# Operand loads, splits and tile rings in the down products of an encoder layer

## The chip, the cores and the metric

The kernel runs on one core of a Trainium2 chip. The metric is the device time of one execution in microseconds; the time before is the median of three runs. Beside the runs one execution is profiled, and every trace row in this document comes from such an execution. Engines are named as in the rows: PE is TensorE's matmul and PEld its weight load, DVE is Vector, ACT is ScalarE, POOL is GpSimd, SP is the queue from which most loads are issued.

## What is computed

One step of a hybrid encoder layer, in float32, on 1024 prompt tokens and 32 sample tokens with D = 1024. The part that the change touches is the last one, the MLP:

```
h = rms_norm(x, g_mix);  z = h @ w_in          # q, k, v, conv, gates
x = x + (sigmoid(ga) * (attn @ w_attn_out) + sigmoid(gb) * (conv @ w_conv_out)) @ w_mix_out
x = x + cross_attention(rms_norm(x, g_cross), 256 memory tokens) @ w_co
x = x + square(relu(rms_norm(x, g_mlp) @ w_up)) @ w_down      # w_up 1024 x 4096, w_down 4096 x 1024
y = rms_norm(x, g_final)
```

## The kernel before, in words

**Three matmuls for one.** Float32 accuracy is reached by parts: every operand x is split into hi, a rounded copy made by ScalarE, and lo = x − hi, made by Vector; each product is then wh·hi + wh·lo + wl·hi, three matmuls of 128 x 128 weights by 264 columns. A weight block of 128 x 1024 is loaded on the SP queue, copied by ScalarE (L131) and subtracted by Vector (L132); this happens two blocks ahead of the step that uses it (`LOOK = 2`, L125), with three buffers.

**The order of the work.** The kernel lists its work as items (`item`, L120), and a planner puts the instructions of each engine in an order, by where they stand in the list and by its own estimate of when their inputs are ready. An instruction wrapped in `pin` (L99) is kept behind the instruction of its engine that was listed just before it. Operand splits are pinned; the splits of weights and the additions of results are not.

**The down product.** It is made of Strassen-like products with seven operands, in this order: b11, t2, b21, n3, n4, n1, b22. Five of them are *half products* (`stage`): eight steps, each one column block j of the result and one half t of the 16 operand blocks; a step has 48 matmuls. The order of the steps is `steps` (j outer, t inner) or `paired` (two j for one t, then the same two for the other t). With t = 1 a result is complete and is added to the sums of x by `to_x1` (Vector, L1908, or GpSimd, L1906). The other two, b21 and n4, are *quarter products* (`stage2`): each is split once more into seven products P1, P6, P2, P7, P5, P4, P3, in this order, with two steps of 24 matmuls each, 14 steps (L2101 to L2103). The first results are kept by a copy (L2052), later ones are added (L2054, L2059).

**What a quarter product needs.** For each of eight pairs k of operand blocks, while the half product ahead of it runs (t2 for b21, n3 for n4):

- `fetch_two`: two loads of 264 KB on GpSimd's own DMA queue (L1692, L1695);
- `first_sums`: three sums on GpSimd (L1701, L1702, L1703);
- `first_split`: the operands of P1 and P7, two ScalarE copies (L1708), two Vector subtractions (L1709);
- `extra_split`: the operands of P6 and P4, one copy (L1712) and one subtraction (L1713) of full width, 128 x 528.

`prepare` lays these over the eight steps of that half product: loads of two pairs at each of the steps 0 to 3, sums one step later, first splits two steps later, extra splits at steps 5 to 7. In the quarter product itself `beside(n)` adds, to step n: the last sums on GpSimd (L1722, for P5), the splits of the second operands for P2 and P3 (`second_split2`, on Vector, L1356, or by `far_split` on GpSimd, L1676), the splits for P5 (`last_split`), and from step 5 on the loads and splits for the next half product (`pump2`, L1678; splits L1355 and L1356). In the other half products `pump2` is called at each step.

**Tiles.** 64 homes of 128 x 528 hold the operands. `free` is a queue of homes: `take_slot` takes the first, `drop` gives one back at the end. In the kernel before every home is a buffer of its own, named by its place (`Z.3`, `H.7`).

Of the kernel before, what the change touches and what calls it, by code (L numbers as in the profile page):

```python
# [40 lines left out]
def hybrid_step(ctx: ExitStack, tc: tile.TileContext, io):  # L41
# [1227 lines left out]
    def open_first():  # L1269

        closed(m_cm)
        S["l"] = ctx.enter_context(tc.tile_pool(name="first", bufs=1, reuse_waits="tile"))
        S["z"] = ctx.enter_context(tc.tile_pool(name="second", bufs=1, reuse_waits="tile"))
        for f in range(NF):
            z = zslot()
            xa[1][f] = (quarter(z, 0), quarter(z, 1))
            pool_e.dma_start(xa[1][f][1].bitcast(F32)[:, : CH[0][1] - QT], xn_d[:, f, QT : CH[0][1]])
        for name in ("w_cq", "w_co"):
            del kept[name, 1]

    def open_sums():
        closed(cr_cm)
        closed(Y["cm", 1])
        S["s"] = ctx.enter_context(tc.tile_pool(name="sums", bufs=1, reuse_waits="tile"))
        for kind in ("t2", "n1", "n3", "n4"):
            for k in range(4):
                comb[kind, k] = tuple(at_slot(f"{kind}.{2 * k + i}") for i in range(2))
# [11 lines left out]
    def open_second():  # L1299
# [3 lines left out]
        S["b"] = ctx.enter_context(tc.tile_pool(name="b22", bufs=1, reuse_waits="tile", side="right"))  # L1303
# [3 lines left out]
    def at_slot(place, dt=F32R):  # L1307
        tag, i = place.split(".")
        pool = S[{"b22": "b", "Z": "z", "lt": "l", "H": "h"}.get(tag, "s")]
        return pool.tile([P, HT], dt, tag=tag + i, bufs=1, name=nm(tag))  # L1310

    turns = {"Z": 0, "lt": 0}

    def next_slot(tag, n, dt):
        turns[tag] += 1
        return at_slot(f"{tag}.{(turns[tag] - 1) % n}", dt)

    def zslot(dt=F32R):
        return next_slot("Z", 8, dt)

    def lslot(dt=F32):
        return next_slot("lt", 4, dt)
# [102 lines left out]
    def second_b22():  # L1425
        for k in range(4):
            comb["b22", k] = tuple(at_slot(f"b22.{2 * k + i}") for i in range(2))
# [218 lines left out]
    places = lambda text: [f"{tag}.{i}" for tag, n in (x.split("*") for x in text.split()) for i in range(int(n))]  # L1646
# [68 lines left out]
    def extra_split(kind, k):  # L1715
        cut(*take_pair(kind, ("e", k)), two["r", k])

    def last_sums(kind, m):
        two["f", m] = f = take_slot((kind, "rf", m), F32)
        for q in range(2):  # L1720
            k = 2 * m + q
            pool_e.tensor_tensor(quarter(f, q), quarter(two["x", k].bitcast(F32), 1), quarter(two["r", k], 0), op=ALU.subtract)  # L1722
            drop((kind, "r", k))
# [16 lines left out]
    def open_down():  # L1740
# [4 lines left out]
        S["h"] = ctx.enter_context(tc.tile_pool(name="hpool", bufs=1, reuse_waits="tile"))  # L1745
# [243 lines left out]
    def prepare(kind):  # L1989

        at = {n: [] for n in range(8)}
        for n in range(4):
            for k in (2 * n, 2 * n + 1):
                at[n].append(lambda k=k: fetch_two(kind, k))
                at[n + 1].append(lambda k=k: first_sums(kind, k))
                at[n + 2].append(lambda k=k: first_split(kind, k))
        for k in range(8):
            at[5 + (k + 1) // 3].append(lambda k=k: extra_split(kind, k))
        return at

    def stage(kind, w, then, q=None, each=None, more=None):
        nxt = KINDS.index(kind) + 1
        at = prepare(KINDS[nxt]) if nxt < len(KINDS) and KINDS[nxt] in RAW2 else None
        order = paired if at or kind in after2 else steps
        if nxt < len(KINDS) and not at:
            item(lambda: wanted2.extend((KINDS[nxt], k) for k in range(16)))
        for n, (j, t) in enumerate(order):

            def fn(ws, n=n, j=j, t=t):
                prod(kind, j, t, then, q)(ws)  # L2010
                if nxt < len(KINDS) and all(x[1] != t for x in order[n + 1 :]):
                    drop_pairs(kind, range(8 * t, 8 * t + 8))
                pump2(4 if n == 0 and kind in after2 else 0 if at else 3)
                for x in at[n] if at else ():
                    x()
# [8 lines left out]
        if nxt < len(KINDS):  # L2024
            item(lambda: pump2(0))

    def stage2(kind, h, f0, last):
# [46 lines left out]
        def beside(n):  # L2074
            if n < 2:
                last_sums(kind, 2 * n)
                last_sums(kind, 2 * n + 1)
            if n < 4:
                second_split2(kind, 2 * n, False)
                second_split2(kind, 2 * n + 1, n > 0)  # L2080
            elif n < 6:
                last_split(kind, 2 * n - 8)
                last_split(kind, 2 * n - 7)
            if n == 5:
                wanted2.extend((nxt, k) for k in range(16))
            if n >= 5:
                pump2({5: 2, 7: 2, 9: 2, 11: 2, 13: 4}.get(n, 0))
# [154 lines left out]
```

## Time and profile before

| what | value |
|---|---|
| runs | 1770.3, 1775.59, 1780.19 us; median 1775.59 |
| the profiled execution, its own time | 1777.22 us |
| its span in the trace | 1775.4 us |
| granted TensorE clock, mean | 0.991 |
| PE busy | 1733.3 us, 98% of the span, 12166 matmuls |
| DVE busy | 1256.8 us, 71% |
| ACT busy | 882.4 us, 50% |
| POOL busy | 773.2 us, 44% |
| the down products | 1408.5 to 1765 us |

The profiled execution's own time is 1.8 us more than its span. A row of a trace gives an instruction's start, its length, the engine, the line of the kernel, the operation, the output and inputs by their names in the program, their shapes and how many it stands for; in brackets is how long the engine stood idle just before and what it waited for. Rows that begin with an engine and end with three numbers are waits by line: total us, times, longest us. In rows with a stretch of time (A:B) come the busy time of each engine, with the number of its instructions, and the clock that TensorE was granted (1.00 is full speed).

### The profile page before, as it was taken

The page shows a single profiled execution, that of the slowest core. Times are in us where ns is not written, and L with a number is a line of the kernel's source. Part 1 is how long each engine was busy: PE and PEld are TensorE (multiplying, and loading weights), DVE is VectorE, ACT ScalarE, POOL GpSimd, SP SyncE. Part 2 cuts the span into 40 slices and gives each one's busy share as a digit, 9 for nine tenths or more (in the row PEclk, how much of TensorE's full clock was granted, in tenths as well). Part 3 has the DMA queues.
Part 4 walks back from the last instruction along what each step waited for, and adds up shares of the span by engine and source line. Part 5 has one row for each costly group of instructions (what it writes and reads, how often), then busy time and mean ns, then how long its engine had stood idle before and what let it go on. Part 6 is the DMA issues. An engine that isn't in the chain of part 4 may idle for free. (4 is left out here: it accounts for less than half of the span.)

```text
span 1775.4 us, 32859 instructions
## 1 busy us (share of the span) xinstructions
PE 1733.3 (98%) x12166; PEld 1708.7 (96%) x12166; DVE 1256.8 (71%) x2322; ACT 882.4 (50%) x1716; POOL 773.2 (44%) x901
## 2 busy tenths in 40 slices
PE   9999999999999999999999999999999999998998
PEld 8999999999999999999999999999999999897998
DVE  7776877868777546656776878686666675866785
ACT  8643534435335324434565666764444543444553
POOL 0026577664673555652324150015555315466221
PEclk9999999999999999999999999999999999998999
DMA  5334445455456888877865667756666775564944
GB/s 185 109 103 140 159 152 189 162 181 173 172 187 238 273 306 286 286 242 263 274 212 196 205 220 240 250 194 219 221 222 218 259 262 174 177 222 136 329 147 146
DMA packets 189009, 369.70 MB, mean 208 GB/s; under 512 B 19617, under 2 KB 108353, under 8 KB 188721
## 3 DMA queue, kind: packets, MB, share of 16 engines
q1 hardware_dynamic: 165232, 287.71, 48.9%
q0 software_dynamic: 22992, 79.12, 13.3%
q8 instruction: 96, 1.57, 0.4%
q10 hardware_dynamic: 624, 0.77, 0.1%
q14 instruction: 65, 0.52, 0.1%
HBM read 265.41 MB, written 101.53 MB: 207 GB/s over the span
## 5 line engine op out<-in xcount | busy, mean ns | idle before, releaser
L131 ACT CAST wh<-wr 128x1024 fp32r<-128x1024 f32 (+1 forms) x226 | 236.2, 1046 | 320.8 <-PE acc L206 82.4
L132 DVE TENSOR_TENSOR wl<-wr,wh 128x1024 fp32r<-128x1024 f32 (+1 forms) x226 | 296.3, 1312 | 99.7 <-ACT wh L131 98.7
L205 PE MATMUL acc<-X,wh 128*128 128x384 f32 (+1 forms) x864 | 281.4, 326 | 0.0
L206 PE MATMUL acc<-X,wh 128*128 128x384 f32 (+1 forms) x864 | 278.7, 323 | 0.0
L207 PE MATMUL acc<-X,wl 128*128 128x384 f32 (+1 forms) x864 | 277.8, 322 | 0.0
L206 PEld LDWEIGHTS acc<-X,wh 128*128 128x128 f32 x864 | 162.7, 188 | 1.3 <-DVE X L285 0.3
L205 PEld LDWEIGHTS acc<-X,wh 128*128 128x128 f32 x864 | 162.4, 188 | 0.8
L207 PEld LDWEIGHTS acc<-X,wl 128*128 128x128 f32 x864 | 162.4, 188 | 0.1
L205 PE MATMUL acc<-Y,wh 128*128 128x384 f32 (+1 forms) x432 | 140.6, 326 | 5.0 <-DVE ct L1093 3.5
L281 POOL TENSOR_TENSOR xacc<-xacc,ct 128x384 f32<-128x384 f32 (+1 forms) x56 | 72.8, 1303 | 160.2 <-ACT ct L279 158.5
L206 PE MATMUL acc<-Y,wh 128*128 128x384 f32 (+1 forms) x432 | 140.0, 324 | 0.2 <-DVE Y L816 0.2
L207 PE MATMUL acc<-Y,wl 128*128 128x384 f32 (+1 forms) x432 | 139.9, 324 | 0.1
L762 POOL TENSOR_TENSOR xacc<-xacc 128x256 f32<-128x256 f32 x132 | 113.6, 860 | 30.1 <-DMA xacc<-in_w_down 22.8
L762 POOL TENSOR_TENSOR ws<-ws 128x256 f32<-128x256 f32 x132 | 112.2, 850 | 29.6 <-DMA ws<-in_w_down 17.4
L131 ACT CAST PTh<-pt 128x512 fp32r<-128x512 f32 (+3 forms) x94 | 46.0, 517 | 101.8 <-PE pt L603 100.3
L205 PEld LDWEIGHTS acc<-Y,wh 128*128 128x128 f32 x432 | 81.7, 189 | 6.5 <-DVE ct L1093 4.3
L206 PEld LDWEIGHTS acc<-Y,wh 128*128 128x128 f32 x432 | 81.7, 189 | 0.9 <-DVE Y L816 0.9
L207 PEld LDWEIGHTS acc<-Y,wl 128*128 128x128 f32 x432 | 81.8, 189 | 0.4 <-DMA wl<-wl_d 0.4
L589 ACT ACTIVATE S<-S,nmx 128x257 f32<-128x257 f32 (+1 forms) x132 | 64.2, 488 | 27.6 <-DVE nmx L584 26.5
L1925 PE MATMUL acc<-n,wh 128*128 128x264 f32 x256 | 73.2, 286 | 2.5 <-DVE n L1356 2.5
L905 PE MATMUL acc<-n,wh 128*128 128x264 f32 x256 | 72.8, 284 | 1.0 <-DVE Z L1572 1.0
L907 PE MATMUL acc<-n,wl 128*128 128x264 f32 x256 | 73.0, 285 | 0.0
(628 smaller groups left out, 5833.4 us busy)
## 6 DMA issues: line engine op xcount, KB each, us to landing
wr<-in_w_up SPq DMA_DIRECT2D x53, 512.0 KB, 4.8
wr<-in_w_in SPq DMA_DIRECT2D x52, 512.0 KB, 4.2
wr<-wsum_d SPq DMA_DIRECT2D x40, 512.0 KB, 4.4
wr<-in_w_conv_out SPq DMA_DIRECT2D x24, 512.0 KB, 4.1
wr<-in_w_mix SPq DMA_DIRECT2D x24, 512.0 KB, 4.8
wr<-in_w_down SPq DMA_DIRECT2D x20, 512.0 KB, 4.6
n_d<-Z SPq DMA_DIRECT2D x32, 264.0 KB, 4.1
xacc<-in_w_down POOLq DMA_DIRECT2D x16, 512.0 KB, 3.8
```

Source lines behind the costliest of these rows:

```text
L131: act.copy(hi, src)
L132: dve.tensor_sub(lo, src, hi.bitcast(F32))
L205: pe.matmul(out, wh[:, a], hi, start=(k == 0), stop=False)
L206: pe.matmul(out, wh[:, a], lo, start=False, stop=False)
L207: pe.matmul(out, wl[:, a], hi, start=False, stop=(k == len(acts) - 1))
L281: pool_e.tensor_tensor(acc, acc, sq, op=ALU.add)
L589: act.activation(stl[:, h, : nk + 1], stl[:, h, : nk + 1], AF.Exp, scale=-1.0, bias=nmx[:, h : h + 1], accum_out=den[:, h : h + 1],)
L762: pin(pool_e.tensor_tensor(t[:, to], t[:, x], t[:, y], op=op))
L905: pe.matmul(acc, wh[:, a], hi, start=(start and k == 0), stop=False, skip_group_check=True)
L907: pe.matmul(acc, wl[:, a], hi, start=False, stop=(k == 3), skip_group_check=True)
L1925: pe.matmul(a, wh[:, s], lo, start=False, stop=False, skip_group_check=True)
```

## The change

- **Rings.** The pools `first`, `second`, `sums`, `b22` and `hpool` become rings of 4, 8, 8, 8 and 12 tiles under one tag each; a home names its ring, not its place in it, and the names of the places and their turns go away. The bytes are the same.
- **b11 in pairs.** The first half product takes the order `paired`.
- **Loads.** `prepare` issues the loads of four pairs at step 0, of two at step 1 and of two at step 2. The sums and first splits keep their steps. An extra split is done by quarters: the first quarter (128 x 264) at steps 6 and 7 of the half product, four pairs in each; the second quarter at steps 4 and 5 of the quarter product.
- **Splits ahead of results.** In t2 and n3, and in n4's and b21's successors n1 and n3, `aside`, which holds `pump2` and the work of `prepare`, is listed ahead of `prod`, and so ahead of the addition of a step's results. In the quarter products `beside(n)` is listed ahead of the next weight's split and of the results of the step.
- **In the quarter product.** The last sums are pinned; every second split of odd k goes to GpSimd (four in place of three); the splits for P5 move from steps 4 and 5 to 6 and 7; `pump2` takes its loads two by two at steps 5 and 8 to 12, none at 6, 7 and 13.

```diff
-        S["l"] = ctx.enter_context(tc.tile_pool(name="first", bufs=1, reuse_waits="tile"))
-        S["z"] = ctx.enter_context(tc.tile_pool(name="second", bufs=1, reuse_waits="tile"))
+        S["l"] = ctx.enter_context(tc.tile_pool(name="first", bufs=4, reuse_waits="tile"))
+        S["z"] = ctx.enter_context(tc.tile_pool(name="second", bufs=8, reuse_waits="tile"))
...
-        S["s"] = ctx.enter_context(tc.tile_pool(name="sums", bufs=1, reuse_waits="tile"))
+        S["s"] = ctx.enter_context(tc.tile_pool(name="sums", bufs=8, reuse_waits="tile"))
...
-                comb[kind, k] = tuple(at_slot(f"{kind}.{2 * k + i}") for i in range(2))
+                comb[kind, k] = tuple(at_slot(kind) for _ in range(2))
...
-    def at_slot(place, dt=F32R):
-        tag, i = place.split(".")
+    def at_slot(tag, dt=F32R):
         pool = S[{"b22": "b", "Z": "z", "lt": "l", "H": "h"}.get(tag, "s")]
-        return pool.tile([P, HT], dt, tag=tag + i, bufs=1, name=nm(tag))
-
-    turns = {"Z": 0, "lt": 0}
-
-    def next_slot(tag, n, dt):
-        turns[tag] += 1
-        return at_slot(f"{tag}.{(turns[tag] - 1) % n}", dt)
+        return pool.tile([P, HT], dt, tag=tag, name=nm(tag))
...
-    places = lambda text: [f"{tag}.{i}" for tag, n in (x.split("*") for x in text.split()) for i in range(int(n))]
+    places = lambda text: [tag for tag, n in (x.split("*") for x in text.split()) for _ in range(int(n))]
...
-    def extra_split(kind, k):
-        cut(*take_pair(kind, ("e", k)), two["r", k])
+    def extra_split(kind, k, q):
+        hi, lo = take_pair(kind, ("e", k)) if q == 0 else dn[kind, ("e", k)]
+        cut(quarter(hi, q), quarter(lo, q), quarter(two["r", k], q))
+        if q:
+            drop((kind, "r", k))
 
     def last_sums(kind, m):
         two["f", m] = f = take_slot((kind, "rf", m), F32)
         for q in range(2):
             k = 2 * m + q
-            pool_e.tensor_tensor(quarter(f, q), quarter(two["x", k].bitcast(F32), 1), quarter(two["r", k], 0), op=ALU.subtract)
-            drop((kind, "r", k))
+            pin(pool_e.tensor_tensor(quarter(f, q), quarter(two["x", k].bitcast(F32), 1), quarter(two["r", k], 0), op=ALU.subtract))
 
     def last_split(kind, m):
         cut(*take_pair(kind, ("f", m)), two["f", m])
...
         closed(L["cm"])
         closed(L["cm2"])
         third.update(n=0, pool=W["pool"])
-        S["h"] = ctx.enter_context(tc.tile_pool(name="hpool", bufs=1, reuse_waits="tile"))
+        S["h"] = ctx.enter_context(tc.tile_pool(name="hpool", bufs=12, reuse_waits="tile"))
 
 
     def cross_units(c):
...
     def prepare(kind):
 
         at = {n: [] for n in range(8)}
-        for n in range(4):
-            for k in (2 * n, 2 * n + 1):
-                at[n].append(lambda k=k: fetch_two(kind, k))
-                at[n + 1].append(lambda k=k: first_sums(kind, k))
-                at[n + 2].append(lambda k=k: first_split(kind, k))
-        for k in range(8):
-            at[5 + (k + 1) // 3].append(lambda k=k: extra_split(kind, k))
+
+        def do(n, fn, ks, *args):
+            at[n] += [lambda k=k: fn(kind, k, *args) for k in ks]
+
+        pairs = [range(2 * i, 2 * i + 2) for i in range(4)]
+        do(0, fetch_two, range(4))
+        do(1, fetch_two, pairs[2])
+        do(2, fetch_two, pairs[3])
+        for i in range(4):
+            do(1 + i, first_sums, pairs[i])
+            do(2 + i, first_split, pairs[i])
+        for i in range(4):
+            do(6 + i // 2, extra_split, pairs[i], 0)
         return at
 
     def stage(kind, w, then, q=None, each=None, more=None):
         nxt = KINDS.index(kind) + 1
         at = prepare(KINDS[nxt]) if nxt < len(KINDS) and KINDS[nxt] in RAW2 else None
-        order = paired if at or kind in after2 else steps
+        order = paired if at or kind in ("b11", *after2) else steps
         if nxt < len(KINDS) and not at:
             item(lambda: wanted2.extend((KINDS[nxt], k) for k in range(16)))
         for n, (j, t) in enumerate(order):
 
             def fn(ws, n=n, j=j, t=t):
+                def aside():
+                    pump2(4 if n == 0 and kind in after2 else 0 if at else 3)
+                    for x in at[n] if at else ():
+                        x()
+
+                early = at or kind in after2
+                if early:
+                    aside()
                 prod(kind, j, t, then, q)(ws)
                 if nxt < len(KINDS) and all(x[1] != t for x in order[n + 1 :]):
                     drop_pairs(kind, range(8 * t, 8 * t + 8))
-                pump2(4 if n == 0 and kind in after2 else 0 if at else 3)
-                for x in at[n] if at else ():
-                    x()
+                if not early:
+                    aside()
                 if behind and (j, t) == (1, 0):
                     behind.pop()()
 
...
                 item(lambda j=j: each(j))
             if more and (j, t) == (1, 0):
                 item(more)
-        if nxt < len(KINDS):
+        if nxt < len(KINDS) and not at:
             item(lambda: pump2(0))
 
     def stage2(kind, h, f0, last):
...
                 drop_pairs(kind, range(8, 16))
 
         def beside(n):
+            two_ks = lambda i: (2 * i, 2 * i + 1)
             if n < 2:
-                last_sums(kind, 2 * n)
-                last_sums(kind, 2 * n + 1)
+                for m in two_ks(n):
+                    last_sums(kind, m)
             if n < 4:
-                second_split2(kind, 2 * n, False)
-                second_split2(kind, 2 * n + 1, n > 0)
+                for k in two_ks(n):
+                    second_split2(kind, k, k % 2)
             elif n < 6:
-                last_split(kind, 2 * n - 8)
-                last_split(kind, 2 * n - 7)
+                for i in two_ks(n - 4):
+                    for k in two_ks(i):
+                        extra_split(kind, k, 1)
+            elif n < 8:
+                for m in two_ks(n - 6):
+                    last_split(kind, m)
             if n == 5:
                 wanted2.extend((nxt, k) for k in range(16))
             if n >= 5:
-                pump2({5: 2, 7: 2, 9: 2, 11: 2, 13: 4}.get(n, 0))
+                pump2({6: 0, 7: 0, 13: 0}.get(n, 2))
 
         n = 0
         for p in order:
...
                         pe.matmul(a, wh[:, s], hi, start=(p in start and k == 0), stop=False, skip_group_check=True)
                         pe.matmul(a, wh[:, s], lo, start=False, stop=False, skip_group_check=True)
                         pe.matmul(a, wl[:, s], hi, start=False, stop=(k == 7), skip_group_check=True)
+                    beside(n)
                     issue_w()
                     if i:
                         ended_with(p)
                     after(p, i)
-                    beside(n)
 
                 item(fn, weights[p](i))
                 n += 1
```

More of the change, by code (lines that the diff above doesn't have):

```diff
@@ L1302, in open_second @@
         closed(ps_cm)
-        S["b"] = ctx.enter_context(tc.tile_pool(name="b22", bufs=1, reuse_waits="tile", side="right"))
+        S["b"] = ctx.enter_context(tc.tile_pool(name="b22", bufs=8, reuse_waits="tile", side="right"))
         L["cm2"], L["pool2"] = opened("late2", bufs=1, reuse_waits="tile", side="right")
         ps = ctx.enter_context(tc.tile_pool(name="ps2", bufs=1, space=PSUM, reuse_waits="tile"))
-    def at_slot(place, dt=F32R):
-        tag, i = place.split(".")
+    def at_slot(tag, dt=F32R):
         pool = S[{"b22": "b", "Z": "z", "lt": "l", "H": "h"}.get(tag, "s")]
-        return pool.tile([P, HT], dt, tag=tag + i, bufs=1, name=nm(tag))
-    turns = {"Z": 0, "lt": 0}
-    def next_slot(tag, n, dt):
-        turns[tag] += 1
-        return at_slot(f"{tag}.{(turns[tag] - 1) % n}", dt)
+        return pool.tile([P, HT], dt, tag=tag, name=nm(tag))
     def zslot(dt=F32R):
-        return next_slot("Z", 8, dt)
+        return at_slot("Z", dt)
     def lslot(dt=F32):
-        return next_slot("lt", 4, dt)
+        return at_slot("lt", dt)
     def lt():
@@ L1426, in second_b22 @@
         for k in range(4):
-            comb["b22", k] = tuple(at_slot(f"b22.{2 * k + i}") for i in range(2))
+            comb["b22", k] = tuple(at_slot("b22") for _ in range(2))
             sp.dma_start(raw("b22", k), xn_d[:, k + 4, HT:])
```

## The prediction

> **What bounds the kernel now.** I read the shares of the engines first, then the busy time by stretches of the down products, then what TensorE waited for there.
>
> ```profile
> PE 1733.3 (98%) x12166; PEld 1708.7 (96%) x12166; DVE 1256.8 (71%) x2322; ACT 882.4 (50%) x1716; POOL 773.2 (44%) x901
> ```
>
> TensorE is the bound, and the change takes no matmul away: it can only win back TensorE's stalls. The stretches, in order: the start of b11, the rest of b11 with t2, the quarter product b21, n3, the quarter product n4. Behind each length stand busy time and instructions of TensorE, its weight loads, Vector, ScalarE and GpSimd, then the granted clock, the DMA engines' share and GB/s.
>
> ```profile
> 1415.70:1430.00 14.30, 11.37 (x77) 10.74 (x76) 11.87 (x14) 8.79 (x14) 3.58 (x2) 0.88 1.05 370
> 1430.00:1513.20 83.20, 83.20 (x684) 83.20 (x683) 57.68 (x127) 33.69 (x55) 30.25 (x43) 1.00 0.58 190
> 1513.20:1565.60 52.40, 46.48 (x356) 43.74 (x355) 38.19 (x54) 27.27 (x39) 19.94 (x19) 1.00 0.69 224
> 1565.60:1610.20 44.60, 44.60 (x368) 44.60 (x368) 27.68 (x42) 18.82 (x33) 31.23 (x40) 1.00 0.59 189
> 1610.20:1670.30 60.10, 49.25 (x356) 46.55 (x355) 46.18 (x66) 31.63 (x48) 29.34 (x27) 0.91 0.63 209
> ```
>
> An unbroken stretch gives the pace: 44.60 / 368 = 0.1212 us per matmul. Three stretches are longer than their matmuls: A, the start of b11, by 14.30 − 77 × 0.1212 = 5.0 us; B, b21, by 52.40 − 356 × 0.1212 = 9.25; C, n4, by 60.10 − 43.15 = 16.95. The sum, 31.2 us, is the ceiling of what this change can win; the two other stretches have no loss. What ended TensorE's waits from 1409 to 1765 us (total, times, longest):
>
> ```profile
> PE acc L2102 <- DVE lt L1709: 6.1, 1, 6.1
> PE acc L2103 <- DVE wl L132: 2.5, 7, 0.6
> PE acc L1925 <- DVE n L1356: 2.5, 2, 1.4
> PE acc L1926 <- DVE wl L132: 2.0, 3, 0.8
> PE acc L1924 <- ACT wh L131: 1.1, 1, 1.1
> PE acc L2101 <- ACT n L2052: 1.0, 1, 1.0
> PE acc L2102 <- DVE b L1713: 1.0, 1, 1.0
> PE acc L2102 <- DVE n L1356: 0.9, 1, 0.9
> ```
>
> One wait is a third of C: in the first step of n4, TensorE stood until a split of an operand of the first quarter product (L1709) was done. The second half of the loss is the clock that it left behind.
>
> ```profile
> 1425.00:1429.00 4.00, 3.53 (x17) 3.32 (x17) 3.11 (x5) 1.72 (x3) 0.00 (x0) 0.57 1.07 354
> 1621.00:1627.00 6.00, 5.80 (x26) 5.72 (x27) 6.00 (x13) 1.27 (x4) 2.63 (x3) 0.51 0.04 11
> ```
>
> ```profile
> 1619.14 0.59 PE L2102 MATMUL acc<-lt,wh 128*128 128x264 f32 x1 [6.08 <-DVE lt L1709]
> ```
>
> After 6.08 us of standing still, 26 matmuls took 6.00 us at a granted clock of 0.51 where the pace gives 3.15: 2.85 us more. In A 17 took 4.00 where 2.06 is the pace: 1.94 more, after gaps of some 1 us each.
>
> **The change, part by part.**
>
> *Operands of a quarter product fetched earlier (GpSimd).* The split that came late stands behind GpSimd's chain of n3: four issues of loads, a landing, six sums, four times over.
>
> ```profile
> 1569.23 0.57 POOL L1692 DMA_DIRECT2D H<-n_d  x1
> ...
> 1575.53 1.28 POOL L1701 TENSOR_TENSOR ct<-H,H 128x264 f32<-128x264 f32 x1 [2.89 <-DMA H<-n_d]
> ...
> 1613.60 1.18 POOL L1703 TENSOR_TENSOR Z<-b,Z 128x264 f32<-128x264 f32 x1
> ```
>
> ```profile
> POOL ct L1701 <- DMA n<-n_d: 6.2, 3, 3.6
> ```
>
> ```profile
> L1277 POOL DMA_DIRECT2D Z<-xn_d x8: 542/542/600, 1057.0 to 1060.7; - x8
> ...
> DMA to landing us min/median/max: 2.3/3.3/4.6
> ```
>
> It runs from 1569.2 to 1614.8, 45.6 us for four rounds, and in them GpSimd stands for landings, 2.89 us and 6.2 in three more: 9.1 us that it could have spent on other sums. The change issues eight loads in step 0, four in step 1, four in step 2: the same 16 issues of 0.57 us and 24 sums, but every landing after the first is now covered by a round of sums (six by 0.9 to 1.3, 5.4 to 7.8 us), and the first in part by the four issues behind it. Eight loads in a row are no risk: another line of this kernel issues eight, and the last row above has them landing in 4.6 us at most. So the chain takes 45.6 − 9.1 = 36.5 us and ends near 1605.7; the splits behind it (L1709, 0.97 us each, below) end near 1608, 2 us before n4's first matmul at 1610.2. Then the 6.1 us, the 2.85 of half clock and the wait for an L1713 split (1.0) go: **C −10**. If L2103's small waits, which stand in the half clock's stretch too, fall with it, one more; if the chain gains only half of its 9.1, it ends at 1610.2, the splits by 1613, and half of the stall is left: bounds −5 and −11. In b21 nothing is won by it: the list has no second L1709 wait.
>
> *Extra splits by quarters, and splits ahead of the results.* Vector was doing these beside the first step of n4:
>
> ```profile
> 1610.73 0.43 DVE L1709 TENSOR_TENSOR Z<-Z,n 128x264 fp32r<-128x264 f32 x1 [5.93 <-POOL lt L1702]
> ...
> 1613.49 0.69 DVE L1713 TENSOR_TENSOR t<-n,Z 128x528 fp32r<-128x528 f32 x1
> 1614.11 1.24 DVE L1713 TENSOR_TENSOR t<-n,t 128x528 fp32r<-128x528 f32 x1
> ...
> 1616.44 1.75 DVE L132 TENSOR_TENSOR wl<-wr,wh 128x1024 fp32r<-128x1024 f32 x1
> 1618.12 0.97 DVE L1709 TENSOR_TENSOR lt<-lt,b 128x264 fp32r<-128x264 f32 x1
> ```
>
> The eight extra splits (L1713) are halved in the half product (first quarter only) and the other halves move to steps 4 and 5 of the quarter product, six steps ahead of P4 which reads them; eight instructions more on ScalarE and on Vector (0.43 to 0.97 us each, as L1709 of that size), which Vector hides: it was busy 38.19 of 52.40 us in B. Each split now stands one step (24 × 0.1212 = 2.9 us) earlier, ahead of the results. The results come later by at most the splits of one step, two to four of 0.4 to 1.2 us; TensorE's wait at L2101 for one (L2052) is 1.0 us. In B this takes the waits for L1356 (0.9), the 1.0 of L2052 in part, and half of L2103's 2.5: **B −2.5**, bounds 0 and −5.
>
> *More on GpSimd in the quarter products.* Four far splits instead of three, and the eight last sums pinned to steps 0 and 1 ahead of them.
>
> ```profile
> L1676 POOL TENSOR_TENSOR n<-n,Z x2: 1861/2092/2322, 1523.2 to 1528.0; 128x528 fp32r<-128x528 f32 x2
> ...
> L1676 POOL TENSOR_TENSOR n<-n,t x1: 2692/2692/2692, 1629.4 to 1629.4; 128x528 fp32r<-128x528 f32 x1
> ```
>
> ```profile
> 1510.81 2.17 POOL L1722 TENSOR_TENSOR n<-t,t 128x264 f32<-128x264 f32 x2 [15.32 <-PE acc L1925]
> ```
>
> Two sums take 2.17 us, eight 8.7; four far splits 4 × 1.9 to 2.7 = 7.4 to 10.8: the chain is 16 to 19.5 us, and P2 wants the last of them in its first step, 4 steps and 21/24 behind the start: 14.3 us. The sums began 2.4 us ahead of the quarter product (1510.81 against 1513.2), so the last far split ends 13.6 to 17.1 us in: a new wait of 0 to 2.8 us. I take 1 in each: **+2** (0 to +5).
>
> A rule speaks against this part. L1713 of one size took 0.69 us and then 1.24, and L132 1.75 where another took 1.21 (the middle row of the next fence), while GpSimd summed. The Trainium skill, "SBUF — State Buffer", section "Who interferes with whom", has Vector and GpSimd share a port pair by an exclusive lock, so that a Vector operation with two SBUF inputs is held until GpSimd's is done. The trace shows the slowing, 1.8 times, but not a full hold of 1 to 2.7 us. By the rule each of the two more far splits would cost Vector its own length, some 2 us, and the sum would be −11; by the rows it is half of that, which the +2 has room for, and the sum goes by them.
>
> *b11 in pairs.* Its operands of half t=1 (L1355, L1356) are first read in step 2, not step 1, one step (48 × 0.1212 = 5.8 us) later. The stretch's last splits are these:
>
> ```profile
> 1421.45 3.05 DVE L1356 TENSOR_TENSOR n<-n,n 128x528 fp32r<-128x528 f32 x3
> 1424.42 1.21 DVE L132 TENSOR_TENSOR wl<-wr,wh 128x1024 fp32r<-128x1024 f32 x1
> 1425.56 2.55 DVE L1356 TENSOR_TENSOR b<-b,b 128x528 fp32r<-128x528 f32 x4
> ```
>
> Unstalled, step 2 would begin near 1426 (1415.7, and the 84 matmuls of steps 0 and 1 that were left then, by 0.1212) and read its eight operands over 5.8 us; the last split ends at 1428. The two waits of 2.5 us and the half clock's 1.94 go; the weights' splits (L131) stay: **A −4.5**, bounds −2.5 and −5.0. The sums that the last up blocks leave to Vector and GpSimd come one step earlier, into the stretch where Vector is busy 11.87 of 14.30 us; if they hold up a weight's split, it costs one of the L1926 waits more (0.8), inside the bounds. t=0 operands are given back one step earlier, and the stretch behind (83.20 us, all busy) shows nobody waiting for slots.
>
> *Rings of tiles.* The same bytes; the planner may take any free slot. The only cost would be a later release, bounded by 0 and one more wait like the smallest above (0.9 us): 0.
>
> Sum: −10 − 2.5 + 2 − 4.5 = −15. The profiled execution took 1777.22 us by its own time (its span 1775.4), the median of the runs 1775.59, 1.6 lower. 1777.2 − 15 = 1762, on the median's footing **1760**. Its own range: with the bounds, −22.5 in total at best (−11, −5, 0 and −5.0, with 1.5 more of the clock), and −5 − 0 + 5 − 2.5 = −2.5 at worst all at once; half of each way round gives 1752 to 1768.
>
> **The rivals.**
>
> *Vector becomes the limit of the quarter products.* In C Vector was busy 46.18 us; TensorE's matmuls there need 43.15. The change moves eight half splits into that stretch (8 × 0.43 to 0.97 = 3.4 to 7.8 us) and takes about as much out of its start (the L1709 and L1713 rows above, 6 us). If all the rest must be done inside, C ends 3 to 5 us over its matmuls plus the structural waits, and B gains nothing: A −4.5, C −5 (as at its bound above), new waits +2: 1768 on the median's footing. For it: the slowed rows; against it: Vector was also slowed by the very queue behind one late operand.
>
> *The early splits hold up Vector's queue in t2 and n3.* Slower side. The splits of step 2+i are now placed ahead of the results and, where the planner follows, ahead of weight splits. If GpSimd's chain is behind its step, Vector stands at a first split, and behind it the evictions and the wl of the next weights. It did stand 5.93 us for one already (the first L1709 row). A round is four issues (2.3) and six sums (5.4 to 7.8), 7.7 to 10.1 us, a step 5.86: after three rounds the chain is 5.5 to 12.7 us behind, and weights are split two to three steps (12 to 17 us) ahead. From 12 us behind TensorE stands. At the old pace (11.4 us a round) it is 17 behind: a stall of some 6 with 2.85 of half clock, 9 in each of t2 and n3: +18 against −10 of what is left: 1784.
>
> *The change does nothing.* The planner orders by readiness and the pins bind only neighbours, so that GpSimd's queue could come out as before, and 1775.6 stays. Against it: the loads, sums and splits are all pinned in traced order.
>
> **How the numbers follow.** Forecast 0.60, Vector as limit 0.18, queue blocked 0.14, nothing 0.08. A measurement of this kernel tells 0.5% (8.9 us) from no change. Faster by more than that (below 1766.7): 0.6 × 0.93 + 0.18 × 0.35 = 0.62; slower (over 1784.5): 0.14 × 0.5 and a remainder for mishaps of the new order, 0.11; within: 0.27. The likeliest case's own range is 1752 to 1768; for 8 in 10 it reaches to the rivals of 1768 and 1775.6 and into the edge of the slower: 1749 to 1780.
>
> **What would show it.** Right: no L1709 wait at n4's first step, a granted clock of 1.00 through C, GpSimd's last sum of n3 6 us or more ahead of n4, DMA waits at L1701 in the first round alone; C near 47 to 50 us, A under 10.5 for 77 matmuls. Wrong: new waits at L2101 and L2102 on L1676 of over 2 us; waits at L1924 to L1926 for wl or wh within t2 and n3, whose stretches have no loss now; C over 55.

## The result and the profile after

The changed kernel took 1763.32 us (median of 8 runs, 1760.2 to 1767.58), the kernel before 1777.34 in runs beside them (8 runs, 1768.84 to 1782.22): 14.0 us less, a ratio of 0.993 with a 95% interval from 0.9905 to 0.9954. 1760 was forecast, with 1749 to 1780 as the range. The profiled execution took 1763.50 us by its own time, its span is 1761.6.

The same stretches in the changed kernel: the start of b11, the rest of b11 with t2, b21, n3, n4, n1 with b22 (columns as before).

```profile
core 0: us, PE busy (x) PEld busy (x) DVE busy (x) ACT busy (x) POOL busy (x), PEclk, DMA share, GB/s
1400.00:1430.00 30.00, 30.00 (x249) 30.00 (x248) 24.30 (x41) 16.61 (x27) 6.71 (x4) 1.00 1.02 365
1430.00:1501.80 71.80, 71.75 (x589) 71.53 (x588) 54.38 (x115) 28.39 (x51) 32.53 (x43) 1.00 0.57 189
1501.80:1555.60 53.80, 47.65 (x377) 46.04 (x376) 44.13 (x64) 31.92 (x51) 24.19 (x20) 1.00 0.68 224
1555.60:1597.60 42.00, 42.00 (x348) 42.00 (x347) 31.40 (x47) 18.51 (x37) 35.18 (x45) 1.00 0.59 194
1597.60:1658.70 61.10, 50.25 (x377) 48.23 (x376) 49.74 (x69) 31.95 (x51) 24.03 (x22) 0.94 0.64 208
1658.70:1751.00 92.30, 92.30 (x761) 92.30 (x761) 64.36 (x112) 47.60 (x77) 22.28 (x16) 1.00 0.56 184
```

At 0.1212 us a matmul: A lost 5.0 and loses nothing now (249 in 30.00 us). B lost 9.25 and loses 53.80 − 377 × 0.1212 = 8.1. C lost 16.95 and still loses 61.10 − 45.69 = 15.4. So only 7.7 of the 13.8 us by which the span is shorter lie in the stretches that the prediction worked out, and the stretch that was to give 10 gave 1.5. The rest was won ahead of them: 1.7 us ahead of the 6800th matmul, where the engines' order is the same in both kernels and single executions differ by more than that (last section), and 4.6 us in the up half behind it. Two of the prediction's own signs speak against it: C was to be 47 to 50 us, wrong over 55, at a clock of 1.00, and is 61.10 (for 377 matmuls) at 0.94. What ended TensorE's waits in the up half, first before, then after:

```profile
PE acc L907 <- DVE wl L132: 1.0, 1, 1.0
PE acc L905 <- DVE Z L1572: 1.0, 1, 1.0
PE acc L906 <- DVE Z L1356: 0.9, 1, 0.9
PE acc L905 <- ACT lt L1413: 0.6, 1, 0.6
PE acc L905 <- ACT lt L1383: 0.5, 1, 0.5
PE acc L905 <- ACT lt L1402: 0.5, 1, 0.5
```

```profile
PE acc L906 <- DVE Z L1349: 0.9, 1, 0.9
PE pc L905 <- DVE Z L1588: 0.6, 1, 0.6
PE acc L905 <- ACT lt L1376: 0.5, 1, 0.5
```

The first two and the fourth and sixth are gone (3.1 us; a new one of 0.6 came): from the start of the 6800th matmul to that of the 9200th it took 304.9 us before and 300.3 after. In the quarter product n4, TensorE's waits are now these:

```profile
PE acc L2116 <- DVE wl L132: 5.6, 2, 4.9
PE acc L2114 <- DVE ct L2067: 1.7, 1, 1.7
PE acc L2115 <- DVE n L1706: 1.1, 1, 1.1
PE acc L2114 <- ACT b L2060: 1.1, 1, 1.1
```

The 6.1 us for a first split (L1709, now L1702) are gone, and one wait of 4.9 us for the wl of n4's third step stands in their place. GpSimd's chain did what was forecast:

```profile
1558.37 0.57 POOL L1685 DMA_DIRECT2D H<-n_d  x1
...
1594.94 1.61 POOL L1696 TENSOR_TENSOR Z<-b,Z 128x264 f32<-128x264 f32 x1
```

From 1558.4 to 1596.6 it is 38.2 us long where it was 45.6 (36.5 was forecast), and ends 1.2 us ahead of n4's first matmul at 1597.7 (the sign of being right was 6 us or more). But then come the rows that decide, Vector's at n4's start, and below them GpSimd's of the same stretch:

```profile
1602.75 0.99 DVE L1706 TENSOR_TENSOR n<-Z,t 128x264 fp32r<-128x264 f32 x1
1603.66 0.98 DVE L1706 TENSOR_TENSOR n<-Z,n 128x264 fp32r<-128x264 f32 x1
1604.57 0.99 DVE L1706 TENSOR_TENSOR n<-lt,n 128x264 fp32r<-128x264 f32 x1
1605.48 1.53 DVE L1706 TENSOR_TENSOR n<-Z,n 128x264 fp32r<-128x264 f32 x1
1606.93 1.57 DVE L1903 TENSOR_TENSOR Gb<-acc,Gb 128x264 f32<-128x264 f32 x6
1608.42 1.95 DVE L132 TENSOR_TENSOR wl<-wr,wh 128x1024 fp32r<-128x1024 f32 x1
```

```profile
1602.50 0.95 POOL L1718 TENSOR_TENSOR n<-n,Z 128x264 f32<-128x264 f32 x1
1603.41 0.94 POOL L1718 TENSOR_TENSOR n<-n,lt 128x264 f32<-128x264 f32 x1
1604.32 0.95 POOL L1718 TENSOR_TENSOR n<-b,Z 128x264 f32<-128x264 f32 x1
1605.23 1.49 POOL L1669 TENSOR_TENSOR Z<-Z,n 128x528 fp32r<-128x528 f32 x1
```

The two engines take turns: a split starts 0.25 us behind each GpSimd sum, every 0.91 us, and lasts 0.98 where one alone lasts 0.42. Two long rows of splits, the first ones and the extra ones, go through Vector nearly all at that pace, then six results, and the wl that TensorE waited for comes last. The results are not slowed: six with one input in PSUM (L1903) took 1.57 us from 1592.32 on, beside GpSimd's sums, and 1.57 without them (in the kernel with the sums on Vector, below).

### The profile page after: what moved, and what is told of

Same layout as the page of the kernel before. It is cut to its first block, busy times and chain, and to the rows that moved or that the text cites. A ratio compares the mean times of both kernels' runs of the same rounds, so it can differ in the third digit from the quotient of the medians.

```text
span 1761.6 us, 32872 instructions
## 1 busy us (share of the span) xinstructions
PE 1725.4 (98%) x12166; PEld 1704.3 (97%) x12166; DVE 1262.2 (72%) x2336; ACT 884.4 (50%) x1732; POOL 782.0 (44%) x903
## 3 DMA queue, kind: packets, MB, share of 16 engines
q8 instruction: 96, 1.57, 0.4%
## 5 line engine op out<-in xcount | busy, mean ns | idle before, releaser
L131 ACT CAST wh<-wr 128x1024 fp32r<-128x1024 f32 (+1 forms) x226 | 236.3, 1046 | 327.3 <-PE acc L1920 95.2
L131 ACT CAST PTh<-pt 128x512 fp32r<-128x512 f32 (+3 forms) x94 | 45.9, 517 | 105.0 <-PE pt L603 103.6
```

Source lines behind the costliest of these rows:

```text
L131: act.copy(hi, src)
```

## The experiments

All kernels in one view. "Up half" is the time from the start of the 6800th matmul to that of the 9200th in the profiled execution; the columns up to "n4 all" are losses, the time from the first to the last matmul's start less 0.1212 us for each matmul. In b11 with t2 only their own matmuls are taken off; 48 of the up half lie between, so that some 6.4 us are no loss. "b21" and "n4" hold the first 13 of the 14 steps (312 matmuls); the last step stands behind 18 to 38 matmuls of the next half product, and "all" has it too, with these matmuls taken off. "Profiled" is the profiled execution's own time, "median" that of the runs; the ratio is to the kernel before, run on the same chip. A profiled execution can lie well off its median (1760.30 against 1768.54 with the sums on Vector), so losses and medians don't add up.

```
                              up half b11+t2   b21   n4  b21 all n4 all profiled  median   ratio, 95% interval
before                          304.9   11.5   7.0  15.7    9.4   17.1  1777.22
changed kernel                  300.3    6.6   7.1  13.6    8.3   15.6  1763.50  1763.32  0.993   0.9905-0.9954
e1  rings alone                 300.7   16.5   6.2  15.4    7.1   16.4  1775.87  1781.92  1.0021  1.0007-1.0035
e2  pairs alone                 304.4   12.1   6.2  13.7    8.3   17.7  1784.52  1778.36  0.9996  0.9981-1.0011
e3  loads alone                 302.1   11.6   6.7   7.7    8.3   12.3  1771.38  1771.38  0.9956  0.994 -0.9973
c4  pairs, loads                307.8   12.8   6.4   7.9    8.8   10.5  1776.46  1772.39  0.9971  0.9955-0.9988
c1  rings, pairs, loads         301.1    6.5   8.1  12.2    9.7   13.2  1769.70  1764.44  0.9914  0.9893-0.9935
e5  changed, aside late         298.0    6.8   9.6  13.6   10.8   15.0  1769.41  1765.57  0.9934  0.9916-0.9951
e6  changed, beside late        298.9    7.0  10.7  13.3   11.9   14.7  1768.36  1767.77  0.9931  0.9908-0.9955
e7  changed, whole extra splits 298.8    7.4   9.3  13.4   10.6   15.2  1767.99  1768.28  0.9939  0.9917-0.9961
e4  changed, last sums later    298.4    7.3  10.1  10.3   11.3   12.4  1763.84  1766.74  0.9935  0.9919-0.9951
a2  changed, sums on Vector     298.8    6.3   8.9  11.7   10.2   13.4  1760.30  1768.54  0.9945  0.9928-0.9961
c5  c1, sums on Vector          301.0    6.5   8.4   9.8   10.7   10.8  1763.57  1763.78  0.9917  0.9893-0.994
c6  c5, far splits on Vector    298.7    6.4   6.4   9.8    7.6   10.7  1754.04  1756.84  0.9895  0.9875-0.9914
```

### Rings alone

```diff
-        S["z"] = ctx.enter_context(tc.tile_pool(name="second", bufs=1, reuse_waits="tile"))
+        S["z"] = ctx.enter_context(tc.tile_pool(name="second", bufs=8, reuse_waits="tile"))
...
-        return pool.tile([P, HT], dt, tag=tag + i, bufs=1, name=nm(tag))
+        return pool.tile([P, HT], dt, tag=tag, name=nm(tag))
```

and so for the other four pools, as in the change.

> The kernel before with the rings of tiles alone. Between the 6800th and the 9200th matmul (the up half) the changed kernel gained 4.6 us (1704 to 1700 is the whole of its lead there: -1.66 at the 6800th, -6.27 at the 9200th), which the prediction had not in its sum. Theory 'rings': the planner, free to take any slot, orders the up half otherwise, and the waits at L907 for wl (1.0), L905 for Z L1572 (1.0), L1402 and L1413 (1.0 together) go: the up half 3 to 5 us shorter than before, b11's two L1356 waits and n4's 6.1 us wait for L1709 as before, in all -3 to -6 us. Rival 'drift': the lead is the spread of single executions: the up half within 1 us of before, all waits as before, total within 2 us.

The up half is 4.2 us shorter, as the theory had it, and in all ten kernels with rings it took 298.0 to 301.1 us, in the four without 302.1 to 307.8. In the traces every engine works in the same order in all fourteen up to 1084 us, and from there to b11 in one of two orders, one with rings and one without, so that these are ten and four executions of the same work. But the kernel is 0.2% slower: at b11 there is a new wait. TensorE's waits from 1410 to 1450 us, and the copy of weights behind it:

```profile
PE acc L1919 <- DVE wl L132: 4.5, 2, 4.0
PE acc L1918 <- DVE n L1349: 2.4, 2, 1.3
```

```profile
1435.39 1.05 ACT L131 CAST wh<-wr 128x1024 fp32r<-128x1024 f32 x1 [7.29 <-DMA wr<-in_w_down]
```

b11's stall on operands (L1349) stayed, and TensorE then stood 4.0 us for weights whose load landed at 1435.3. What the rings win in the up half they lose there.

### b11 in pairs alone

```diff
-        order = paired if at or kind in after2 else steps
+        order = paired if at or kind in ("b11", *after2) else steps
```

> The kernel before with the paired order of b11 alone. Theory 'pairs': the three waits at b11's start (1.36, 1.10, 0.47 us) and the half clock behind them go, 5.0 us less there and nothing elsewhere: -4 to -5 us. Rival: the stall at b11's start went by the rings, which let operands be loaded and split earlier; then it stays here, within 1 us of before, and goes in the run with rings alone.

Neither. The three waits at b11's start are gone, and some 15 us behind their place there are two others (TensorE from 1425 to 1455 us; ScalarE's copy; a stretch of ten us):

```profile
PE acc L1926 <- DVE wl L132: 2.0, 1, 2.0
PE acc L1924 <- ACT wh L131: 1.8, 1, 1.8
```

```profile
1444.81 1.04 ACT L131 CAST wh<-wr 128x1024 fp32r<-128x1024 f32 x1 [6.26 <-DMA wr<-in_w_down]
```

```profile
1435.00:1445.00 10.00, 9.11 (x75) 8.90 (x73) 6.91 (x20) 2.85 (x5) 0.00 (x0) 1.00 1.05 381
```

The DMA engines are full there (1.05, 381 GB/s), as they are in every kernel for the first 30 us of b11 (shares of 0.98 to 1.07 in stretches of 10 us). The pairs put off what b11 needs of its operands; the weights, on the same full engines, are late next. The prediction gave the operands' wait a price and did not ask what was late behind it.

### The early loads alone

```diff
+        for n, ks in enumerate((range(4), range(4, 6), range(6, 8))):
+            for k in ks:
+                at[n].append(lambda k=k: fetch_two(kind, k))
         for n in range(4):
             for k in (2 * n, 2 * n + 1):
-                at[n].append(lambda k=k: fetch_two(kind, k))
```

> The kernel before with the loads of a quarter product's operands at steps 0 (four pairs), 1 and 2, all else as before. Theory: GpSimd's chain of n3 shrinks from 45.6 us to 36 to 39 and ends before n4's first matmul; the 6.1 us wait for L1709 goes, but Vector then has the splits, the full extra splits and the weights' wl in one queue at n4's start, and a wait for wl of 2 to 5 us comes in its place: n4's stretch 2 to 7 us shorter, in all -2 to -7. As the prediction has it (nothing late behind it): n4's stretch 10 us shorter. Rival: the chain does not shrink, the stretch stays within 2 us.

The theory holds. The chain is 35.6 us long (1568.9 to 1604.5), n4's loss falls from 15.7 to 7.7 in its first 13 steps, and by the runs the part is worth 7.8 us (0.9956). Over the whole of n4 the loss falls only from 17.1 to 12.3. What is left in the first steps is a wait for wl, three times, without the half clock. The wait for wh stands behind them, between n4's 13th step and its last, where the DMA engines are full (1.06 from 1651 to 1666 us), and there the half clock follows (0.72 from 1657 to 1663):

```profile
PE acc L2105 <- DVE wl L132: 3.2, 3, 1.4
PE acc L1924 <- ACT wh L131: 1.8, 1, 1.8
PE acc L2103 <- ACT n L2054: 1.1, 1, 1.1
```

### Pairs and loads; rings, pairs and loads

The two edits above together, and then all three.

> The kernel before with b11 in pairs and the early loads, without rings. Pairs alone traded b11's first stall for one on late weights (loss of b11 with t2 12.1 where it was 11.5), rings alone likewise (16.5), rings, pairs and loads together lost 6.5. Theory 'together': b11 with t2 loses 12 again, n4 8 to 10: 1768 to 1772. Rival: the loads, not the rings, freed b11 beside the pairs; then 6 to 7 are lost there and the time is 1762 to 1766.

> The kernel before with three parts of the change: rings, b11 in pairs, loads of a quarter product's operands at steps 0 to 2. Left out: the new place of the splits, extra splits by quarters, the moved steps of the quarter product. Rings alone moved the time by +0.2%, pairs alone by nothing (each took away a stall at b11's start and got another on late weights), loads alone by -0.4% (n4's loss from 15.7 to 7.7 us). Theory 'the rest gives back': b11's loss goes only with rings and pairs together, n4 loses 7 to 9 us where the changed kernel loses 13.6, so this kernel is faster than the changed one by 4 to 7 us: 1756 to 1761. Rival 'the rest is needed': b11's stall stays here (loss of b11 with t2 11 to 12 us as before), since the place of t2's work frees it in the changed kernel: 1764 to 1770.

Without rings b11 with t2 loses 12.8 us, with rings 6.5: its stall went only where rings and pairs stood together (here with the loads, which without rings did nothing for it; rings and pairs without the loads were not run), and that is worth the 5 us that the prediction gave to the pairs. The DMA engines are as full in the changed kernel (1.02 in its first row above); there the weights that came late with the pairs alone were copied 27.3 us behind b11's first matmul (1429.4, 1402.1), where with the pairs alone it was 30.1 (1444.8, 1414.7), and the copy waited with hardly anyone held (two gaps of 0.2 and 0.1 us on TensorE, 1431.4 to 1432.0):

```profile
1429.40 1.05 ACT L131 CAST wh<-wr 128x1024 fp32r<-128x1024 f32 x1 [3.65 <-DMA wr<-in_w_down]
```

With the three parts the kernel takes 1764.4 us, level with the changed one. The other parts (splits ahead of results, quarters, a fourth far split, moved steps) win nothing that these runs can tell. But the expectation for n4 missed: its first 13 steps lose 12.2 us with rings, 7.7 and 7.9 without. Over the whole of n4 it is 13.2 against 12.3 and 10.5, for without rings the last step loses 4.6 and 2.6, with them 1.0. With rings the planner orders all engines otherwise from the up half on; which difference costs n4 these 1 to 3 us was not settled.

### The places undone in the changed kernel, one by one

```diff
-                early = at or kind in after2
+                early = kind in after2
```

```diff
-                    beside(n)
                     issue_w()
...
                     after(p, i)
+                    beside(n)
```

```diff
-            do(6 + i // 2, extra_split, pairs[i], 0)
+            do(6 + i // 2, extra_split, pairs[i])
...
-                        extra_split(kind, k, 1)
```

Aside late, beside late, and the extra splits whole (128x528, none of them in the quarter product):

> The changed kernel with the work of a quarter product's operands listed behind the results in t2 and n3 again (in n1 and n3's first place as the change has it). Theory 'place': the wl that n4's third step waited for (4.9 us) is then listed ahead of the last half product's extra splits and is done before them, the wait goes, n4's loss falls from 13.6 to 7 to 10 us, in all 4 to 6 us faster than the changed kernel. Rival 'GpSimd holds Vector': the eight extra splits at 0.9 us each stay in the way of something else (L1702 or L1706 waits of 3 to 5 us in P1 or P6): within 2 us of the changed kernel.

> The changed kernel with the work beside the quarter products listed behind a step's weights and results again. The change was costed at -2.5 us in b21 for it; b21 lost 7.0 us before and 7.1 after. If the place is worth nothing: b21's loss stays at 6 to 8 us and the time within 2 us of the changed kernel. If it was worth 2.5 and something else took it back: b21 loses 9 to 10 us. If the place costs, since splits held by GpSimd stand ahead of weights' wl: the two waits of 1.5 and 1.6 us at b21's first steps and the 4.9 in n4 fall, n4 loses 8 to 11 us.

> The changed kernel with the extra splits whole (128x528) at steps 6 and 7 of the half product, none in the quarter product. A split of 128x264 took 0.42 us alone and 0.98 beside GpSimd's sums, one of 128x528 0.70 and 1.25: about 0.56 more, whatever its size. So eight whole ones at n4's start take 9.4 us from one start to the next where eight halves took 7.3. Theory: the wl of n4's third step comes 2 us later, its wait is 6 to 7 us and n4's loss 15 to 16, while the 8 fewer instructions in the quarter product win nothing: +1 to +3 us against the changed kernel. Rival: fewer instructions, fewer holds: 1 to 3 us faster.

Aside late: the wait for wl is 4.88 us, as in the changed kernel; that theory of the place fell. Beside late: b21 loses 10.7 where it lost 7.1, as if splits ahead of the results were worth 3.6 us in b21. But the other kernels that keep them there lose 7.1, 9.6, 9.3, 10.1 and 8.9, each in one execution, so the worth of the place is not shown. In n4 the 4.9 us go and two waits for far splits (1.2 each) come. Whole: waits of 2.3 and 2.3 for wl in place of one of 4.9, n4's loss the same. All three are within the spread of the changed kernel: n4 loses 13.3 to 13.6 whatever the place.

### GpSimd's last sums moved, then taken over by Vector

```diff
-            if n < 2:
-                for m in two_ks(n):
+            if n in (2, 3):
+                for m in two_ks(n - 2):
                     last_sums(kind, m)
```

(In this kernel they read the low parts that the splits leave in the place of the operands, so that P5 multiplies other numbers; the instructions are the same.)

> The changed kernel with GpSimd's eight last sums of a quarter product at steps 2 and 3 in place of 0 and 1; they are read at step 8. In the changed kernel eleven splits of 128x264 in a row take 0.97 to 1.00 us each at n4's start, one per GpSimd sum, where one alone takes 0.42, and the wl of the third step stands behind them: a new wait of 4.9 us with half clock after it. Theory 'port': Vector is held by each GpSimd sum; without the sums there the splits take 0.42 to 0.5 us, the wl comes about 6 us earlier and the wait falls below 1 us: n4's stretch 5 to 8 us shorter than in the changed kernel, 1755 to 1759 us in all. Rival 'place': the splits stand ahead of wl whatever they take, and the chain's last sums are late: wait of 3 to 5 us stays, time within 2 us of the changed kernel. Third: the last sums are then late for the far splits and P2, a new wait of 2 to 5 us there takes back what is won.

The wait of 4.9 us is gone, as "port" has it: with GpSimd still, the same splits took 0.42 each. The third case came too: P2 waits 2.7 us for a split behind the sums, and b21 loses 10.1. The time stayed (1766.7, within the spread of the changed kernel). So the sums were put on Vector, at the same place in the order:

```diff
-            pin(pool_e.tensor_tensor(quarter(f, q), quarter(two["x", k].bitcast(F32), 1), quarter(two["r", k], 0), op=ALU.subtract))
+            pin(dve.tensor_tensor(quarter(f, q), quarter(two["x", k].bitcast(F32), 1), quarter(two["r", k], 0), op=ALU.subtract))
```

> The changed kernel with the eight last sums of each quarter product on Vector in place of GpSimd, at the same place in the order; nothing else moves. Beside GpSimd's sums each Vector split took 0.56 us more, whatever its size (0.42 to 0.98, 0.70 to 1.25, the wl 1.21 to 1.78), and without them 0.42 in a row at n4's start when the sums were moved. Theory 'GpSimd holds Vector': Vector takes on eight sums of some 0.35 us from one start to the next (2.8 us) and is rid of some 14 holds of 0.56 (7.8 us) at n4's start: the wl of the third step is done 4 to 6 us earlier, its wait of 4.9 us falls under 1 us with the half clock behind it, n4's loss from 13.6 to 7 to 9 us, b21's from 7.1 to 5 to 7; 5 to 7 us faster than the changed kernel: 1756 to 1759. Rival 'Vector is simply full': eight more operations in its queue make the wait longer, 6 to 8 us, and the kernel 2 to 4 us slower than the changed one.

Vector at n4's start in this kernel:

```profile
1597.33 0.42 DVE L1706 TENSOR_TENSOR t<-n,t 128x264 fp32r<-128x264 f32 x1
1597.67 0.42 DVE L1706 TENSOR_TENSOR n<-Z,t 128x264 fp32r<-128x264 f32 x1
...
1599.05 1.57 DVE L1903 TENSOR_TENSOR Gb<-acc,Gb 128x264 f32<-128x264 f32 x6
1600.54 1.21 DVE L132 TENSOR_TENSOR wl<-wr,wh 128x1024 fp32r<-128x1024 f32 x1
```

n4's first matmul is at 1597.1 here, at 1597.7 in the changed kernel, so the wl is done 8 us earlier (1601.7 against 1610.4), and no wait for it is left in n4's first steps. Only the engine of the eight sums was changed, Vector's other rows stand in the same order, and the 4.9 us went: that GpSimd held Vector there is shown. The expected gain in time is not: P2 now waits for GpSimd's far splits (1.3 and 1.2), a result in b21 for its place in Vector's queue (3.0), n4 loses 11.7 and b21 8.9, and 1768.5 us (0.9945) is no better than the change. The hold works the other way round too. GpSimd's first far split of n4 in this kernel:

```profile
1602.58 7.21 POOL L1669 TENSOR_TENSOR H<-H,b 128x528 fp32r<-128x528 f32 x1 [8.32 <-ACT n L1668]
```

It took 7.21 us where it took 1.50 in the changed kernel, beside an unbroken row on Vector of sums, wl and splits, which took their usual 0.42, 1.21 and 0.70. It was done 1.2 us after the first instruction of that row with an input in PSUM (a result, L2062, at 1608.55), and P2's wait of 1.3 us ended with it.

### The simpler kernel with GpSimd taken out of the quarter products

The kernel with rings, pairs and loads, its last sums on Vector as above; then the far splits too:

```diff
-                second_split2(kind, 2 * n + 1, n > 0)
+                second_split2(kind, 2 * n + 1, False)
```

> The kernel with rings, b11 in pairs and the early loads alone (median 1764.4; n4's loss 12.2, b21's 8.1 us), with the last sums on Vector. Theory 'GpSimd holds Vector': n4's waits for L1349 (1.7 and 0.9) and wl (1.4) with the half clock go, n4 loses 6 to 8 us, b21 6 to 8: 1757 to 1760, level with the run above or ahead of it by 1 to 2. Rival 'full': slower than 1764 by 2 to 4.

> The kernel with rings, b11 in pairs, the early loads and the last sums on Vector, and now also the far splits on Vector (L1676 in the kernel before), so that GpSimd has no sums or splits beside a quarter product. If what still delays P2 is GpSimd's far splits (0.53 and 0.54 us of waits, 1.1 and 1.0 for Vector's splits that they hold): a split on Vector takes 0.62 us from one start to the next where GpSimd takes 1.3 to 1.8 and holds Vector 1.1; these waits fall under 0.5 each, n4 loses 7 to 9 us where it lost 9.8, b21 6.5 to 8 where it lost 8.4: 1758 to 1762. If Vector is full by now: P2's waits for its own splits grow to 2 to 3 us in each quarter product, 1765 to 1769.

With the sums on Vector n4 loses 9.8 in place of 12.2, and the time stays (1763.8, where 1757 to 1760 was expected). With the far splits too, b21 loses 6.4 where it lost 8.4, the waits for L1669 are gone and the kernel takes 1756.8 us: 0.9895, 0.9875 to 0.9914. n4 stays at 9.8, where 7 to 9 was expected. The time is 20 us under the kernel before and, by the medians, 6.5 under the changed one. But its interval overlaps those of the changed kernel (from 0.9905 on) and of the two kernels that it was made from (0.9914 and 0.9917), so a gain over these is likely and not shown. Its two quarter products (b21, n3, n4):

```profile
1498.10:1550.90 52.80, 48.38 (x374) 46.05 (x374) 40.47 (x65) 28.05 (x40) 8.30 (x10) 1.00 0.70 231
1550.90:1593.20 42.30, 42.30 (x350) 42.30 (x350) 35.58 (x54) 20.88 (x38) 33.47 (x43) 1.00 0.58 196
1593.20:1647.00 53.80, 47.52 (x357) 45.38 (x356) 41.21 (x64) 28.39 (x42) 10.71 (x11) 0.97 0.65 219
```

The stretches of different kernels don't hold the same rows on Vector, so what the moved work costs it is read over the whole down part, from b11's first matmul to b22's last: 259.6 us busy for 425 instructions with rings, pairs and loads, 258.9 for 447 in this kernel, with eight sums and three splits more in each quarter product. It took over the 22 and is no busier.

## Why the prediction was right, and where it was not

The time, its sign and its size came out (−15 forecast, −14.0 measured), but by terms that made up for each other: C gave 1.5 of its 10, and the up half 4.6 that the sum had at 0. That the sum met the forecast is luck. (One working is off as well: half of each way round the forecast would be 1756 to 1766; its 1752 is the whole of the better way.)

- **Loads, C −10.** The chain (38.2 us; 36.5 forecast) and the end of the L1709 wait came as worked out, and alone the part wins 8 us in n4's first 13 steps, 4.8 over the whole of it. In the whole change C gave 1.5. The step that failed is that with the splits done near 1608 the 6.1, the 2.85 and the 1.0 would simply go: it priced the two splits behind the chain at their 0.97 us and left out the row of extra splits, the results and the wl queued behind them on Vector, the splits and the wl each held by GpSimd.
- **More on GpSimd, +2.** The wait was sought in P2, for the far splits; in the changed kernel P2 has none for them. It came at n4's third step, on wl: 4.9 us and half clock. The mis-sized term is the price of GpSimd's work for Vector. The prediction read the rows 0.69 and 1.24 as a slowing, "not a full hold". The runs show a hold per instruction: 0.56 us more for 128x264 (0.42 to 0.98), 0.55 for 128x528 (0.69 to 1.24), 0.54 for the wl (1.21 to 1.75), and nothing where GpSimd's sums are taken away (0.42). In these rows it is not the size of Vector's instruction that matters but the GpSimd instruction beside it: a far split of 128x528 cost a 128x264 split 1.11 (0.42 to 1.53). On this the Trainium skill, "SBUF — State Buffer", section "Who interferes with whom", was right in kind: a Vector instruction with two inputs in SBUF waits for a GpSimd instruction that reads it, and whoever comes first keeps the ports. The prediction had cited it and gone against it.
- **Splits ahead, B −2.5.** B loses 8.1 where it lost 9.25. With the far splits' cost of 1 taken off, −1.5 was forecast for B and −1.1 measured; whether the place did it is not shown (10.7 without it, 7.1 to 10.1 with it, in b21's first 13 steps).
- **Pairs, A −4.5.** The 5.0 came, by rings and pairs together (beside the loads); by either alone nothing. The step that failed is "the weights' splits (L131) stay": with the DMA engines full they are late next.
- **Rings, 0.** They are worth some 5 us in the up half (304.8 is the mean of the four kernels without, 299.5 of the ten with them) and, beside the early loads, cost 1 to 3 in n4 (13.2 against 12.3 and 10.5). The prediction costed a later release; it did not think of the planner laying out the whole down half and part of the up half anew.
- **Rivals.** "Vector becomes the limit" comes closest to what happened in C, though by GpSimd's holds and not by Vector's own work, and without the up half's 4.6 us its 1768 would have been the closer number. "The early splits hold up Vector's queue" was wrong in its place, for t2 and n3 lose nothing (71.75 of 71.80, 42.00 of 42.00), and right in its mechanism: wl behind splits that run at GpSimd's pace.

## What to carry to other kernels

Price a stall by what is queued behind it: here each operand wait that an edit removed had a late weight behind it on the same engine or on the same full DMA engines, and the edit paid in full only where that was early too. Work moved to GpSimd is not free for Vector, nor is halving Vector's instructions beside it: each split or wl beside a GpSimd sum paid some 0.55 us here, so that 22 instructions taken from GpSimd and given to Vector left Vector no busier. Nor is GpSimd's own work safe there: one far split took 7.21 us. And a change of how tiles are named can reorder work far from the place it was meant for, so compare whole traces, not the edited stretch.

## What the runs showed of the hardware that was not expected

The granted clock does not need a long gap. In the last kernel two gaps of 0.46 and 1.02 us, 1.7 us apart, were followed by clock 0.67:

```profile
1604.60 0.39 PE L2097 MATMUL acc<-H,wh 128*128 128x264 f32 x1 [0.46 <-DVE H L1349]
1606.25 0.39 PE L2097 MATMUL acc<-n,wh 128*128 128x264 f32 x1 [1.02 <-DVE n L1349]
```

```profile
1608.00:1612.00 4.00, 4.00 (x25) 4.00 (x24) 1.55 (x4) 0.15 (x1) 0.00 (x0) 0.67 0.41 135
```

25 matmuls in 4.00 us where the pace gives 33. With the loads alone two gaps of 1.44 and 1.45 us, 4.6 us apart, left it at 1.00. So in these two cases short waits close together cost more than their sum and longer ones spread out did not; where the limit lies these runs do not tell. Also, executions differ by up to ten us at the 6800th matmul (1066.6 to 1076.8 us), ahead of everything that was edited (the engines' order is the same in all of them there), so that a single span says little and the stretches behind it have to be read by themselves.
